# Half of one modulation vector's product moved from the attention stage to the output projection

## The chip, the cores and the metric

The kernel runs on one core of a Trainium2 chip. A core has TensorE (matmuls), VectorE, ScalarE, GpSimd and SyncE (called PE, DVE, ACT, POOL and SP in the profile), each with its own queue of instructions that it takes in order, and 16 DMA engines that move data between HBM and the core's on-chip memory. The metric is the device time of one execution in microseconds. Work on different engines overlaps; an instruction that waits holds up what stands behind it in its own queue.

## The reference, cut to what matters

One decoder layer over 256 tokens of width 2048: four groups of attention heads, an output projection, then a mixture of 16 experts of which each token takes two. A vector `c` of the sequence gives six modulation vectors of 2048 numbers each.

```python
c_act = jax.nn.silu(c)
mod = c_act @ ada_w[l] + ada_b[l]
sh1, sc1, g1, sh2, sc2, g2 = jnp.split(mod, 6, axis=-1)
h = rmsnorm(x, norm1_g[l]) * (1.0 + sc1[:, None]) + sh1[:, None]
x = x + g1[:, None] * token_mixer(h, w_in[l], ...)
h = rmsnorm(x, norm2_g[l]) * (1.0 + sc2[:, None]) + sh2[:, None]
x = x + g2[:, None] * moe_ffn(h, router_w, router_bias, ...)
return rmsnorm(x, final_g)
```

`g2` scales what the experts give, so it is wanted last of the six. Its weights are 2048 x 2048 numbers in float32, 16.8 MB.

## The kernel before

All weights are streamed from HBM once, in one list of units of 512 KB (128 partitions x 1024 numbers; the expert gate and up weights in units of 1 MB). The class `Stream` gives each unit a slot in on-chip memory as slots come free (`pump`, `done`) and SP issues the loads. Slots are halves of the ring tiles `r0` to `r4`, a single `r5` and, once attention no longer needs them, the tiles `T` of the position biases and a few more. Names as `ug`, `uo`, `uw`, `ugu` in the profile are such slots, named after the unit that took them first.

The stages follow each other, and the list of units has their order:

1. The vectors `sc1` and `sh1` and the first projections of w_in (until about 158 us).
2. The other projections of w_in, 69 units, and attention for the groups D, C, A and B. A unit of w_in is split into a high part `whi` (ScalarE, line 584) and a low part `wlo` (VectorE, line 586), and three matmuls (lines 561 to 563, or 565 to 567) take the place of one. `order` mixes the units of w_in with those of `sc2`, `sh2` and `g2`, evenly.
3. The output projection: 32 pieces of w_out (`opieces`, counted from 0), split in the same way, two pieces ahead of the matmuls `oacc` (`SPLITS = 2`). `order2` mixes the pieces with the units of `g1`. After every eight pieces, 512 columns of `x` are added up (lines 1190 and 1191); the last 512 columns come in two halves. Then the router picks the experts.
4. Eight pairs of experts, gate, up and down weights. In the first pair, the columns of `g2` are spread to rows of `g2r` by `spread`, among the gate and up matmuls.

A vector in `VEC` is made on VectorE: `ada_acc_v` takes 1024 columns at a time and adds one unit (128 rows of the weight) after another to `ada_v`: the first by a product (line 509), the others by a multiply-add (line 511). `ada_item` calls it for each unit, and after the sixteenth puts the finishing on a list, `late_cols`; `finish_cols` calls `ada_finish`, which sums over the partitions with small matmuls and a transposition (`ada_cols`). A tuple of 16 units is one block, so `sc2`, `sh2` and `g2` make six blocks of 16 units.

The order within each engine's queue is set when the kernel is built: a scheduler takes the instructions as written and places them by a simulated timeline, so a change in the list of units moves neighbours too.

Of the kernel before, what the change touches and what calls it, by code (L numbers as in the profile page):

```python
# [11 lines left out]
F32 = mybir.dt.float32  # L12
# [8 lines left out]
D = 2048  # L21
S = 256
KC = D // 128
# [2 lines left out]
F = 512  # L26
CAP = 64
VEC = {(n, h) for n in ("sc2", "sh2", "g2") for h in range(2)}
TAIL = ("g1",)
NEG = -1e30  # L30
EPS = 1e-6
TINY = float(np.finfo(np.float32).tiny)
# [1 line left out]
UNIT = 1024  # L34
# [146 lines left out]
def hybrid_trunk_kernel(  # L181
# [113 lines left out]
    def ada_blocks(nm):  # L295
        return [k for h in range(2) for k in ([(nm, 2 * h, 1024)] if (nm, h) in VEC else
                                              [(nm, 2 * h, 512), (nm, 2 * h + 1, 512)])]
# [11 lines left out]

    nw = len(wtiles)  # L310
    wkeys = [u[0] for i in range(NEARLY, nw) for u in win_units(i)[3 * (i == SIXTH):]]
    blocks = [k for nm in ("sc2", "g1", "sh2", "g2") if nm not in TAIL for k in ada_blocks(nm)]
    lines = [[(k, u) for k in blocks if k[2] == width for u in range(KC * width // UNIT)] for width in (1024, 512)]
    akeys = [a[1:] for a in sorted(((n + 0.5 * on) / (len(ks) + 1), *ku)
                                   for on, ks in enumerate(lines) for n, ku in enumerate(ks))]
# [16 lines left out]
            units.append(ada_block(it[1])[it[2]])  # L332
    opieces = [(n, u) for n, us in WORDER for u in us]
    order2, fi = [], 0
    akeys2 = [(k, u) for nm in TAIL for k in ada_blocks(nm) for u in range(KC * k[2] // UNIT)]
    for i in range(32):
        order2.append(("o",) + opieces[i])
        while fi < len(akeys2) and fi < 1.2 * i + AHEAD:
            order2.append(("a",) + akeys2[fi])
            fi += 1  # L340
    order2 += [("a",) + k for k in akeys2[fi:]]
    for it in order2:
        units.append(wout_units(it[1])[it[2]] if it[0] == "o" else ada_block(it[1])[it[2]])
# [184 lines left out]
    def spread(cols, dst):  # L528

        pr = ps("PT", [128, 4, 128], name="ada_r")  # L530
        for i in range(4):
            dg = small([128, 128], "dg", bufs=2)
            V.tensor_scalar(dg, ident, cols[:, i:i + 1], None, OP.mult)
            mm(pr[:, i, :], ones[:], dg[:], start=True, stop=True)
        A.copy(dst, pr[:].rearrange("p i n -> p (i n)"))
# [7 lines left out]
    g2c = const.tile([128, KC], F32, name="g2c")  # L543
# [545 lines left out]
    def finish_cols(age):  # L1089
        for c in late_cols:  # L1090
            c[0] += 1
        while late_cols and late_cols[0][0] > age:
            late_cols.pop(0)[1]()
# [5 lines left out]
    for it in order:  # L1099
        if it[0] == "w":  # L1100
            i, u = pieces[pn]
# [44 lines left out]
    late = wrA = bsb = rt = xt = g1b = fa8 = selb = tms = x1q = None  # L1146
# [277 lines left out]
    next(first)  # L1424
    ssy = const.tile([128, 2, 7], F32, name="ssy")
    fgr = []
    for p in range(NP):
        xg = xgs[p // 2]
        gp = ps("mm", [128, 512], name="gatep")
        up = ps("mm", [128, 512], name="upp")  # L1430
        for n, (c, g) in enumerate(GUORDER):
            if n == 5:
                weights(p)
            if p == 0 and n > 3:

                b = n - 4
                if b == 0:
                    g2r = late.tile([128, D], F32, name="g2r", tag="g2r")
                spread(g2c[:, 4 * b:4 * b + 4], g2r[:, 512 * b:512 * b + 512])
            o = (gp, up)[g]  # L1440
            keys = [(("gu", p), c, g, e) for e in range(2)]
            bt = Batch()
            for i in range(4):
                k = 4 * c + i
                if not p and not g and not i % 2:
                    next(first, None)
                if not p or i == 2:
                    bt = Batch()
                for e in (1, 0):
                    w = stream.get(keys[e])[:, 512 * i:512 * i + 512]  # L1450
                    s0 = 2 * CAP * (p % 2) + CAP * e
                    bt(mm, o[64 * e:64 * e + 64, :], xg[:, k, s0:s0 + CAP], w, start=k == 0, stop=k == KC - 1)
            for key in keys:
                stream.done(key)
# [218 lines left out]
```

## Time and profile before

| | |
|---|---|
| median of 3 runs | 1056.02 us (1053.86 to 1061.72) |
| profiled execution | 1056.39 us |
| its span, first to last instruction | 1054.6 us |
| TensorE busy | 960.3 us (91%) |
| VectorE busy | 500.4 us (47%) |
| ScalarE busy | 353.1 us (33%) |
| moved by DMA | 371.14 MB, mean 352 GB/s |

The busy times come from one execution and are averages over stages that differ. Matmuls are pipelined and their ends are modelled, so a busy TensorE isn't TensorE at its peak. The chain of waits is followed back from the last instruction; "issue" in it is time in which an engine waited for nothing that the profile shows. The DMA share is the mean busy share of the 16 DMA engines; it can pass 1.

### The profile page before, as it was taken

The page shows a single profiled execution, that of the slowest core. Times are in us where ns is not written, and L with a number is a line of the kernel's source. Part 1 is how long each engine was busy: PE and PEld are TensorE (multiplying, and loading weights), DVE is VectorE, ACT ScalarE, POOL GpSimd, SP SyncE. Part 2 cuts the span into 40 slices and gives each one's busy share as a digit, 9 for nine tenths or more (in the row PEclk, how much of TensorE's full clock was granted, in tenths as well). Part 3 has the DMA queues.
Part 4 walks back from the last instruction along what each step waited for, and adds up shares of the span by engine and source line. Part 5 has one row for each costly group of instructions (what it writes and reads, how often), then busy time and mean ns, then how long its engine had stood idle before and what let it go on. Part 6 is the DMA issues. An engine that isn't in the chain of part 4 may idle for free.

```text
span 1054.6 us, 16417 instructions
## 1 busy us (share of the span) xinstructions
PE 960.3 (91%) x6465; PEld 582.9 (55%) x6465; DVE 500.4 (47%) x1006; ACT 353.1 (33%) x763; POOL 4.8 (0%) x14
## 2 busy tenths in 40 slices
PE   5899999999999998989998999999889897899994
PEld 1677778898788985656784433433243232433323
DVE  2444566996998998344445231414024040422215
ACT  3333344566776768534444101100010000200013
POOL 0000000000000000000000000000000000000000
PEclk9999999999999999999998999999999999999998
DMA  9999999996999999889653999999999999999994
GB/s 332 357 358 359 357 323 325 355 373 210 335 325 348 325 384 387 307 270 384 228 214 145 341 421 414 412 417 415 422 407 421 412 420 413 419 419 414 421 359 128
DMA packets 153596, 371.14 MB, mean 352 GB/s; under 512 B 11514, under 2 KB 90275, under 8 KB 136875
## 3 DMA queue, kind: packets, MB, share of 16 engines
q1 hardware_dynamic: 152512, 368.41, 94.2%
q10 hardware_dynamic: 938, 1.61, 0.4%
q8 instruction: 53, 0.87, 0.3%
q14 instruction: 29, 0.23, 0.1%
q0 software_dynamic: 64, 0.02, 0.0%
HBM read 367.91 MB, written 2.10 MB: 351 GB/s over the span
## 4 chain that ended last, share of the span: by engine, by line
PE 66%; DMA 15%; DVE 8%; ACT 5%; issue 4%; SPq 0%; DVEq 0%; ACTq 0%
PE dn L201 10%; DMA ugu<-in_exp_w_up_dram 9%; PE acc L561 5%; PE acc L562 4%; PE acc L563 4%; PE gatep L201 4%; PE upp L201 3%; PE ada L201 3%; PE upp L204 3%; DMA r<-in_exp_w_up_dram 3%; PE oacc L565 3%; PE pg L1410 3%; PE oacc L566 3%; PE oacc L567 3%; PE gatep L204 2%
## 5 line engine op out<-in xcount | busy, mean ns | idle before, releaser
L561 PE MATMUL acc<-Hh,wlo 128*128 128x256 f32 x512 | 145.7, 294 | 6.3 <-DVE wlo L586 3.9
L562 PE MATMUL acc<-Hl,whi 128*128 128x256 f32 x512 | 146.1, 288 | 0.0
L563 PE MATMUL acc<-Hh,whi 128*128 128x256 f32 x512 | 145.2, 286 | 0.0
L586 DVE TENSOR_TENSOR wlo<-r,whi 128x1024 fp32r<-128x1024 f32 x85 | 103.8, 1221 | 62.7 <-ACT whi L584 60.1
L584 ACT CAST whi<-r 128x1024 fp32r<-128x1024 f32 x85 | 88.9, 1047 | 77.2 <-PE acc L563 28.7
L561 PEld LDWEIGHTS acc<-Hh,wlo 128*128 128x128 f32 x512 | 96.3, 192 | 16.9 <-DVE wlo L586 7.0
L562 PEld LDWEIGHTS acc<-Hl,whi 128*128 128x128 f32 x512 | 98.6, 193 | 3.5 <-issue 2.6
L563 PEld LDWEIGHTS acc<-Hh,whi 128*128 128x128 f32 x512 | 98.6, 193 | 2.7 <-issue 2.3
L511 DVE SCALAR_TENSOR_TENSOR ada_v<-r,cT,ada_v 128x1024 f32<-128x1024 f32 x75 | 95.9, 1279 | 0.4
L204 PE MATMUL upp<-ugu,xg 128*64 128x512 f32 x220 | 90.7, 597 | 4.4 <-DMA ugu<-in_exp_w_up_dram 4.4
L1464 DVE TENSOR_TENSOR he<-upp,sg 128x128 f32<-128x128 f32 x32 | 7.1, 282 | 180.0 <-PE upp L204 180.0
L204 PE MATMUL gatep<-ugu,xg 128*64 128x512 f32 x192 | 82.2, 601 | 0.5 <-DMA ugu<-in_exp_w_gate_dram 0.5
L1543 ACT CAST yhl<-yo 128x512 fp32r<-128x512 f32 x31 | 19.1, 618 | 164.1 <-DVE yo L1537 136.8
L204 PE MATMUL gatep<-r,xg 128*64 128x512 f32 x176 | 71.1, 596 | 0.9 <-DMA r<-in_exp_w_gate_dram 0.9
L201 PE MATMUL dn<-udh,heT 128*64 128x512 f32 x140 | 68.0, 599 | 1.0 <-DVE heT L1481 1.0
L1494 DVE TENSOR_TENSOR xt<-xt,sco 128x512 f32<-128x512 f32 (+1 forms) x70 | 42.1, 637 | 55.4 <-PE sco L1493 54.9
L204 PE MATMUL upp<-r,xg 128*64 128x512 f32 x148 | 65.7, 596 | 2.6 <-DMA r<-in_exp_w_up_dram 2.6
L204 PE MATMUL dn<-udh,heT 128*64 128x512 f32 x140 | 67.6, 599 | 0.0
L1460 ACT ACTIVATE sg<-gatep 128x512 f32<-128x512 f32 x8 | 4.8, 597 | 167.9 <-PE gatep L204 167.9
L565 PE MATMUL oacc<-wlo,Oh 128*128 128x512 f32 (+1 forms) x160 | 58.8, 369 | 0.2
L201 PE MATMUL dn<-r,heT 128*64 128x512 f32 (+1 forms) x124 | 55.5, 558 | 1.6 <-DVE heT L1481 1.6
L567 PE MATMUL oacc<-whi,Oh 128*128 128x512 f32 (+1 forms) x160 | 56.8, 355 | 0.0
(404 smaller groups left out, 1909.0 us busy)
## 6 DMA issues: line engine op xcount, KB each, us to landing
r<-in_ada_w_dram SPq DMA_DIRECT2D x156, 512.0 KB, 7.6
udh<-in_exp_w_down_dram SPq DMA_DIRECT2D x70, 512.0 KB, 11.4
r<-in_w_in_dram SPq DMA_DIRECT2D x69, 512.0 KB, 7.3
ugu<-in_exp_w_up_dram SPq DMA_DIRECT2D x34, 1024.0 KB, 14.6
ugu<-in_exp_w_gate_dram SPq DMA_DIRECT2D x33, 1024.0 KB, 13.8
r<-in_exp_w_gate_dram SPq DMA_DIRECT2D x31, 1024.0 KB, 13.0
r<-in_exp_w_up_dram SPq DMA_DIRECT2D x30, 1024.0 KB, 14.3
r<-in_exp_w_down_dram SPq DMA_DIRECT2D x56, 512.0 KB, 11.4
```

Source lines behind the costliest of these rows:

```text
L201: ins = op(*args, **kw).ins
L204: ins = op(*args, **kw).ins
L511: V.scalar_tensor_tensor(acc, w, cT[:, u:u + 1], acc[:], OP.mult, OP.add)
L561: ins = mm(o, wl, hh, start=first, stop=False)
L562: mm(o, wh, hl, start=False, stop=False)
L563: mm(o, wh, hh, start=False, stop=last)
L565: ins = mm(o, hh, wl, start=first, stop=False)
L566: mm(o, hl, wh, start=False, stop=False)
L567: mm(o, hh, wh, start=False, stop=last)
L584: A.copy(hi, w)
L586: V.tensor_tensor(lo, w, hi[:].bitcast(F32), OP.subtract)
L1494: V.tensor_tensor(y(t, cs), y(t, cs), o, OP.add)
```

## The change

`g2` has two blocks of 1024 columns. The first block (columns 0 to 1023) leaves `order` and enters `order2`: its 16 units follow the pieces of w_out with the numbers 18 to 31, one or two behind each (`G2FROM = 17`). The second block stays where it was. The finishing of the late block is called in the first pair of experts, ahead of the spreading, and the four rows of `g2r` are spread in the order 2, 3, 0, 1.

```diff
-TAIL = ("g1",)
+TAIL = ("g1", "g2")
+G2FROM = 17
...
-    blocks = [k for nm in ("sc2", "g1", "sh2", "g2") if nm not in TAIL for k in ada_blocks(nm)]
+    blocks = [k for nm in ("sc2", "sh2") for k in ada_blocks(nm)] + ada_blocks("g2")[1:]
...
-    akeys2 = [(k, u) for nm in TAIL for k in ada_blocks(nm) for u in range(KC * k[2] // UNIT)]
+    akeys2 = [(k, u) for k in ada_blocks("g1") for u in range(KC * k[2] // UNIT)]
+
+    g2keys = [[(k, u) for u in range(KC)] for k in ada_blocks("g2")]
+    gi = 0
     for i in range(32):
         order2.append(("o",) + opieces[i])
         while fi < len(akeys2) and fi < 1.2 * i + AHEAD:
             order2.append(("a",) + akeys2[fi])
             fi += 1
+        while gi < KC * (i - G2FROM) / (31 - G2FROM):
+            order2.append(("a",) + g2keys[0][gi])
+            gi += 1
...
+    def g2_row(b):
+
+        spread(g2c[:, 4 * b:4 * b + 4], g2r[:, 512 * b:512 * b + 512])
+
...
+            if p == 0 and n == 4:
+                finish_cols(0)
+                g2r = late.tile([128, D], F32, name="g2r", tag="g2r")
             if p == 0 and n > 3:
-
-                b = n - 4
-                if b == 0:
-                    g2r = late.tile([128, D], F32, name="g2r", tag="g2r")
-                spread(g2c[:, 4 * b:4 * b + 4], g2r[:, 512 * b:512 * b + 512])
+                g2_row((2, 3, 0, 1)[n - 4])
```

The lines of the changed kernel have other numbers: 511 is 518 there, 586 is 593, 1190 and 1191 are 1197 and 1198.

First place: SP's queue at the start of the mixed stage, behind the units for the compression in group D. Before (`in_ada_w` with 128x1024 is a unit of `sc2`, `sh2` or `g2`, `in_w_in` one of w_in):

```order
L219 DMA r_96<-in_ada_w_dram 128x1024
L219 DMA r_97<-in_ada_w_dram 128x1024
L237 DMA r_97<-in_w_in_dram 128x4x256
L219 DMA r_98<-in_ada_w_dram 128x1024
L219 DMA r_94<-in_ada_w_dram 128x1024
L237 DMA r_98<-in_w_in_dram 128x4x256
```

Now, in the same place:

```order
L220 DMA r_96<-in_ada_w_dram 128x1024
L238 DMA r_97<-in_w_in_dram 128x4x256
L220 DMA r_97<-in_ada_w_dram 128x1024
L238 DMA r_98<-in_w_in_dram 128x4x256
L220 DMA r_94<-in_ada_w_dram 128x1024
```

Between two units of w_in there is now one unit of the modulation weights where there were two; over the whole stage 80 of 96 are left.

Second place: VectorE's queue in the output projection, from the split of piece 24 to that of piece 28. Before (two `wlo` in a row stand as x2: those of 23 and 24, 25 and 26, 27 and 28; `work` and `xt` are the additions to `x`):

```order
L586 TENSOR_TENSOR wlo<-uo_5467,whi 128x1024 x2
L1190 TENSOR_TENSOR work<-oacc,g1b 128x512 x2
L1191 TENSOR_TENSOR xt<-xt,work 128x512 x2
L586 TENSOR_TENSOR wlo<-r_98,whi 128x1024 x2
L586 TENSOR_TENSOR wlo<-uo_5534,whi 128x1024 x2
```

Now:

```order
L593 TENSOR_TENSOR wlo<-ug_5536,whi 128x1024
L518 SCALAR_TENSOR_TENSOR ada_v<-uo_5563,cT,ada_v 128x1024
L1197 TENSOR_TENSOR work<-oacc,g1b 128x512 x2
L518 SCALAR_TENSOR_TENSOR ada_v<-r_95,cT,ada_v 128x1024
L593 TENSOR_TENSOR wlo<-uo_5563,whi 128x1024
L1198 TENSOR_TENSOR xt<-xt,work 128x512 x2
L518 SCALAR_TENSOR_TENSOR ada_v<-ug_5589,cT,ada_v 128x1024
L593 TENSOR_TENSOR wlo<-r_97,whi 128x1024
L518 SCALAR_TENSOR_TENSOR ada_v<-ug_5596,cT,ada_v 128x1024
L593 TENSOR_TENSOR wlo<-ug_5589,whi 128x1024
L518 SCALAR_TENSOR_TENSOR ada_v<-r_95,cT,ada_v 128x1024
L518 SCALAR_TENSOR_TENSOR ada_v<-r_98,cT,ada_v 128x1024
```

Six of the late sums now stand between these splits, three of them between the splits of pieces 24 and 26, and two in a row ahead of that of piece 28.

Third place: SP's queue at the end of the output projection, up to the first up weights of the experts. Now (the rows of w_out are the last four pieces; before, no row of `in_ada_w` stood among or behind them):

```order
L246 DMA r_96<-in_w_out_dram 128x4x256
L220 DMA ug_5589<-in_ada_w_dram 128x1024
L246 DMA ug_5589<-in_w_out_dram 128x4x256
L246 DMA r_97<-in_w_out_dram 128x4x256
L246 DMA r_94<-in_w_out_dram 128x4x256
L220 DMA ug_5596<-in_ada_w_dram 128x1024
L220 DMA ug_5664<-in_ada_w_dram 128x1024
L260 DMA ug_5664<-in_exp_w_down_dram 128x1024
L220 DMA r_95<-in_ada_w_dram 128x1024
L220 DMA r_96<-in_ada_w_dram 128x1024
L257 DMA ugu_5693<-in_exp_w_up_dram 128x2048
```

Four units of `g2` are the last loads before the experts' up weights, the first of which stood among the pieces of w_out before.

## Rows read from the trace of the kernel before

**Rows 1.** From the profile page: the span, and the busy tenths of TensorE, VectorE and the DMA engines with the GB/s moved, in 40 equal slices of the span (26.4 us each).

```profile
span 1054.6 us, 16417 instructions
...
PE   5899999999999998989998999999889897899994
...
DVE  2444566996998998344445231414024040422215
...
DMA  9999999996999999889653999999999999999994
GB/s 332 357 358 359 357 323 325 355 373 210 335 325 348 325 384 387 307 270 384 228 214 145 341 421 414 412 417 415 422 407 421 412 420 413 419 419 414 421 359 128
```

**Rows 2.** Busy time of each engine by stage: the stretch, its length in us, then us busy (and instructions) of PE, PE's weight loads, DVE, ACT and POOL, the granted clock, the DMA share and GB/s.

```profile
158.00:211.00 53.00, 51.43 (x510) 44.86 (x499) 43.11 (x84) 27.04 (x56) 1.05 (x2) 1.00 1.00 341
211.00:264.00 53.00, 52.33 (x435) 46.03 (x435) 40.98 (x80) 34.02 (x85) 0.00 (x0) 1.00 0.85 291
264.00:422.00 158.00, 147.88 (x1152) 126.53 (x1151) 143.02 (x261) 110.25 (x272) 0.00 (x0) 0.98 1.00 351
422.00:475.00 53.00, 50.12 (x316) 31.07 (x315) 22.18 (x60) 24.59 (x57) 1.68 (x3) 0.93 0.85 288
475.00:527.00 52.00, 52.00 (x270) 37.23 (x269) 23.06 (x25) 23.48 (x37) 0.00 (x0) 1.00 0.85 308
527.00:557.00 30.00, 25.22 (x207) 23.62 (x205) 16.20 (x47) 14.71 (x28) 0.00 (x0) 0.93 0.56 210
557.00:606.00 49.00, 48.40 (x234) 22.69 (x236) 18.60 (x44) 13.79 (x23) 0.00 (x0) 0.94 0.67 244
606.00:1015.00 409.00, 373.15 (x1702) 140.93 (x1699) 102.75 (x197) 35.87 (x61) 0.00 (x0) 1.00 1.02 416
```

**Rows 3.** Two consecutive matmuls of TensorE's timeline in the attention stage: start us, us, engine, line, operation, tiles and shapes.

```profile
330.23 0.28 PE L567 MATMUL acc<-whi,Hh 128*128 128x256 f32 x1
330.35 0.28 PE L565 MATMUL acc<-wlo,Hh 128*128 128x256 f32 x1
```

**Rows 4.** The chain of waits by engine and line, as shares of the stretch: from 158 to 422 us, from 264 to 422 us, and from 475 to 557 us.

```profile
by line: issue 11.5%; PE acc L561 9.0%; PE acc L562 8.0%; PE acc L563 7.9%; DVE ada_v L511 5.8%; DVE wlo L586 4.8%; DMA r<-in_w_in_dram 4.8%; PE acc L565 4.8%; PE acc L566 4.3%; PE acc L567 4.3%; ACT whi L584 4.1%; PE PT L204 2.9%; PE sp L2
...
by line: issue 15.5%; DMA r<-in_w_in_dram 8.1%; DVE ada_v L511 7.1%; ACT whi L584 6.2%; PE acc L561 6.0%; PE acc L562 5.2%; PE acc L563 5.2%; DVE wlo L586 5.0%; DMA r<-in_ada_w_dram 3.2%; PE acc L565 2.8%; DMA uw<-in_w_in_dram 2.8%; PE PT L
...
by line: PE oacc L565 24.4%; PE oacc L566 22.7%; PE oacc L567 22.7%; PE g1p L1065 4.9%; PE ada L201 4.3%; PE PT L1203 3.2%; PE rt L1209 2.6%; PE g1p L1064 2.3%; ACT xh L1369 1.6%; ACT L1297 1.6%; PE lg L1232 1.0%; DVE dg L533 1.0%; PE ada_r
```

**Rows 5.** The instructions that write or read the tile `ada_v`, over the whole span: count, then minimum, median and maximum in ns, the first and the last start in us, and the shapes.

```profile
L511 DVE SCALAR_TENSOR_TENSOR ada_v<-r,cT,ada_v x75: 1254/1279/1286, 150.5 to 409.4; 128x1024 f32<-128x1024 f32 x75
...
L522 DVE STREAM_TRANSPOSE ada_v<-ada_c x6: 443/450/450, 199.9 to 431.5; 128x256 f32<-128x256 f32 x6
...
L509 DVE TENSOR_SCALAR ada_v<-r,cT x5: 744/752/753, 146.8 to 374.9; 128x1024 f32<-128x1024 f32 x5
...
L523 DVE TENSOR_TENSOR A2n<-ada_v,rT x2: 168/169/170, 200.4 to 254.3; 128x8 f32<-128x8 f32 x2
```

**Rows 6.** From the profile page: the loads of the modulation weights that went to ring slots, their number, KB each, and median us from issue to landing.

```profile
r<-in_ada_w_dram SPq DMA_DIRECT2D x156, 512.0 KB, 7.6
```

**Rows 7.** SP's timeline in the output projection: the first loads of `x` and the last pieces of w_out (start us, us until the last of the group was issued).

```profile
467.02 3.06 SPq L1183 DMA_DIRECT2D xt<-in_x_dram  x6
...
498.18 1.74 SPq L245 DMA_DIRECT2D uo<-in_w_out_dram  x2
```

**Rows 8.** VectorE's timeline from the split of piece 24 to that of piece 30; in brackets the idle time before an instruction, and what ended it.

```profile
519.69 1.23 DVE L586 TENSOR_TENSOR wlo<-uo,whi 128x1024 fp32r<-128x1024 f32 x1 [1.50 <-ACT whi L584]
520.84 1.28 DVE L1190 TENSOR_TENSOR work<-oacc,g1b 128x512 f32<-128x512 f32 x2
522.03 1.28 DVE L1191 TENSOR_TENSOR xt<-xt,work 128x512 f32<-128x512 f32 x2
523.24 1.22 DVE L586 TENSOR_TENSOR wlo<-r,whi 128x1024 fp32r<-128x1024 f32 x1
525.35 1.22 DVE L586 TENSOR_TENSOR wlo<-r,whi 128x1024 fp32r<-128x1024 f32 x1 [0.90 <-ACT whi L584]
529.04 1.22 DVE L586 TENSOR_TENSOR wlo<-uo,whi 128x1024 fp32r<-128x1024 f32 x1 [2.46 <-ACT whi L584]
532.67 1.23 DVE L586 TENSOR_TENSOR wlo<-uo,whi 128x1024 fp32r<-128x1024 f32 x1 [2.41 <-ACT whi L584]
533.81 0.42 DVE L1190 TENSOR_TENSOR work<-oacc,g1b 128x256 f32<-128x256 f32 x1
534.48 0.42 DVE L1190 TENSOR_TENSOR work<-oacc,g1b 128x256 f32<-128x256 f32 x1 [0.24 <-PE oacc L567]
534.82 0.75 DVE L1191 TENSOR_TENSOR xt<-xt,work 128x256 f32<-128x256 f32 x2
535.55 1.23 DVE L586 TENSOR_TENSOR wlo<-r,whi 128x1024 fp32r<-128x1024 f32 x1
538.23 0.42 DVE L1229 COPY work<-PT 128x256 f32<-128x256 f32 x1 [1.45 <-PE PT L1227]
539.14 1.22 DVE L586 TENSOR_TENSOR wlo<-uo,whi 128x1024 fp32r<-128x1024 f32 x1 [0.48 <-ACT whi L584]
```

**Rows 9.** Who waited for whom: VectorE's longest wait from 475 to 548 us, and SP's from 475 to 575 us (us in total, times, longest).

```profile
DVE wlo L586 <- ACT whi L584: 35.7, 14, 5.4
...
SPq L256 <- DVE wlo L586: 27.5, 7, 6.3
```

## The prediction

> **What bounds the kernel now.** The page comes first. TensorE is busy for 91% of the span and the DMA row shows a 9 in nearly every slice; the slices that don't are the tenth and those from the 17th to the 22nd, and the GB/s line has its holes there [rows 1]. The table by stage puts figures on them [rows 2]. From 158 to 422 us (projections and attention) the transfers run at a share of 0.85 to 1.00, VectorE is busy for 227 of 264 us and TensorE for 95%. That 95% isn't a limit: matmuls of this stage have records of 0.28 us and start 0.12 us apart [rows 3], so busy records overlap and hide waits. From 422 to 557 us (output projection, router) transfers fall to 288, 308 and 210 GB/s and VectorE is busy for 45% of the time. From 606 us on (the experts) transfers run at 416 GB/s with a share of 1.02, to the end.
>
> The chain of waits says who sets the pace [rows 4]. In attention no engine does: matmuls, "issue", the sums of `ada_v`, the splitting into `wlo` and `whi`, and transfers take turns. From 264 to 422 us alone, transfers are 8.1 + 3.2 + 2.8 = 14.1% of the chain and `ada_v` is 7.1%. From 475 to 557 us some 70% of the chain is the `oacc` matmuls: TensorE sets the pace, and VectorE waits for ScalarE's split, which waits for TensorE (35.7 us in 14 waits) [rows 9].
>
> So the same work is on the path, in part, where the change takes it from, and beside it where the change puts it, if it fits.
>
> **What leaves the attention stage.** Of six blocks of 16 early sums one goes: one opening product of 0.75 us and 15 sums of 1.279 us [rows 5], 0.75 + 15 x 1.279 = 19.9 us of VectorE. With them go 16 transfers of 512 KB [rows 6], 8.39 MB. On the path are only parts of both:
> - Sums: `ada_v` is 5.8% of the chain over 264 us [rows 4], 15.3 us; a sixth of the sums go, so 2.6 us.
> - Transfers: 14.1% of 158 us is 22.3 us of chain from 264 us on. If these waits shrink with the bytes (8.39 of the stage's 337 GB/s x 264 us = 89 MB, 9.4%; the rate is from the stage table's first three rows), 2.1 us go. If each landing comes earlier by all that is no longer ahead of it, all 22.3 us can go. Queues near their limit shorten faster than their load, which speaks for more than 2.1; the 15.5% "issue" and the splits in the same chain, which stay, speak for far less than 22.3. I take 6 us.
> - Bounds for both together: nothing, if the split-multiply loop keeps its pace; 25 us, if transfers alone set it (8.39 MB at 337 GB/s).
>
> Gain taken: 2.6 + 6 = 8.6 us.
>
> **What enters the output projection.** VectorE gets the 19.9 us here: two of the sums ahead of the split of piece 12, the other 14 behind the splits of pieces 16 to 29. A split `wlo` can start only when ScalarE's `whi` is there, and the idle time before each shows what fits [rows 8]. Taking the new order of VectorE's rows against those gaps: a sum of 1.28 us fits into idle 1.50, 2.46 and 1.45 + 0.48. It doesn't fit around 520 to 525 us, where the four additions of `work` and `xt` fill the gap: three sums stand there against 0.90 idle, 3 x 1.28 - 0.90 = 2.9 us over. Two sums in a row against 2.41 are 0.15 over. One sum beside the additions of 533.81 to 535.55 us, with 0.24 idle among them, is 1.04 over, less one addition of 0.37 us (half of the last pair) that now comes later: 0.7. TensorE waits for each of these, since its next piece needs `wlo`. Cost: 3.8 us. Bounds: nothing, if the two buffers of `wlo` take up the delay; 19.9 us, if every sum delays a split.
>
> The finishing of this half (a transposition of 0.45 us and an addition of 0.17 us [rows 5], after eight small matmuls) leaves a busy stage and now stands between the last addition and the router's first reduction on VectorE: 0.6 us, on the path. Bounds: nothing and about 1.5 us with the wait for the matmuls.
>
> The transfers: SP issues 14 of the 16 units behind the loads of `x`, mixed with the last 12 pieces of w_out, ahead of all expert weights but the first gate pair and one down unit. They cost nothing here if they land before VectorE reaches them. The cover is the hole: from 475 to 557 us transfers stay under the experts' rate by (416 - 308) x 52 + (416 - 210) x 30 = 11.8 MB, and SP mostly waits there for a slot (27.5 us for `wlo`) [rows 2, 9]. 14 units are 7.3 MB. Without that cover they would cost 8.39 MB / 416 GB/s = 20.2 us. Expert weights are prefetched later, into slots that come free by the last split as before; the first pair of experts starts then, with the same slots full. `spread` makes the same four rows of `g2r` in another order: nothing.
>
> **The sum.** The profiled execution took 1056.39 us (span 1054.6, 1.8 around it), 0.4 above the median of the runs. 1056.4 - 8.6 + 3.8 + 0.6 = 1052.2: **1052 us**.
>
> **Rivals.**
> - *Attention is limited by its transfers.* For it: shares of 1.00 from 158 to 211 and from 264 to 422 us, beside 1.02 where the experts stream, and SP far from idle. Then the units that leave (16 in 264 us, 12.8 of them in these 211 us) give back their transfer time, 12.8 x 0.524 MB / 348 GB/s = 19 us: 1056.4 - 19 + 4.4 = 1042 us. Against it: 416 GB/s in the expert stage shows that the engines move more than 351. A rule of the Trainium skill (DMA: Bandwidth & Descriptors, Specifications) gives one core's share of HBM as about 358 GB/s and calls that side the binding one; by it attention sits at the ceiling and 8.39 MB would be worth 23 us, an estimate from that page. The 416 GB/s of this trace contradict it as a ceiling. Chance 0.23.
> - *Attention keeps its pace.* The loop of split, `wlo` and matmul, with TensorE at 95%, is the limit, and what leaves was waiting beside it: 1056.4 + 4.4 = 1061 us. For it: "issue" and matmuls are over half of the chain. Against: 14% of the chain are transfers. Chance 0.15.
> - *The late sums wait for their data* (the slower side). VectorE takes its rows in order; a sum whose unit hasn't landed holds the split behind it, and so TensorE and every slot that SP waits for. From the first loads of `x` on, at 467 us [rows 7], the change queues 30 units of 512 KB, 2.1 MB of gates, 2.1 MB of `x` and one down unit of 0.5 MB: 20.4 MB, wanted by the split at 539 us, so 283 GB/s. The stage before ran at 288 and the next at 308 [rows 2]; the margin is thin. At 250 GB/s the queue needs 82 us, 10 too many: 1062. At 210 GB/s, the rate of 527 to 557 us, it needs 97, 25 too many: 1077. It decides below about 234 GB/s, where the queue comes 15 us late and the time passes 1067. Against it: these rates are low because slots weren't free (in the kernel before, the last piece is issued at 498 us, and SP then waits for splits [rows 7, 9]), and a summed unit frees its slot at once. Chance 0.15.
>
> That the change doesn't do what it says is excluded by the order: 80 of the 96 sums are early, 16 late.
>
> **Chances.** Forecast 0.47, rivals 0.23, 0.15, 0.15. One per cent is 10.6 us, about what a measurement of this kernel can tell from no change. Faster by over 1% (under 1046): most of the first rival (0.20) and the good edge of my case (0.08), 0.28. Slower by over 1% (over 1067): 0.13 of the third rival and 0.01 of the second, 0.14. Within: 0.58. The range reaches from 1041, just under the first rival's value, to 1064, past the second rival and into the third; half of the first rival's chance and most of the third's lie outside.
>
> **What would show it.** Right: 80 `ada_v` operations in attention and 16 late; what now stands at 422 us comes near 413; transfers are a smaller part of its chain; pieces 16 to 29 take some 4 us more, with VectorE near 85% busy; transfers over 350 GB/s from 475 to 557 us; the experts' stretch keeps its 409 us at 416 GB/s. Wrong on the gain: the chain of attention keeps its length and shows "issue" or ScalarE where transfers were. Wrong on the cost: `ada_v` waits for a transfer between 500 and 545 us, `oacc` matmuls show idle time before them put down to `wlo`, or the first expert pair waits for up weights, which are now the last to be issued before it.

## The result: slower by 1.1%, and the profile after

The changed kernel took 1068.19 us (median of 4 runs, 1066.15 to 1071.15), the kernel before 1055.95 us beside it (4 runs). The ratio is 1.0108, with a 95% interval of 1.0079 to 1.0137. The forecast was 1052 us with a range up to 1064; the change made the kernel slower, and by more than the range allowed. The profiled execution of the changed kernel took 1067.70 us, its span 11.0 us more than before.

From the page of the changed kernel, the rows that answer to [rows 1] (slices of 26.6 us):

```profile
span 1065.6 us, 16414 instructions
...
PE   5999999799999998989998998999789998899885
...
DMA  9999998698699997879983999999999999999992
GB/s 336 358 359 358 357 312 282 223 371 271 190 348 342 374 357 269 294 231 398 384 316 141 342 421 415 417 419 406 423 412 411 412 419 416 416 420 414 421 377 102
```

The eighth slice (186 to 213 us) is new: 223 GB/s where there were 355, and TensorE's digit falls to 7. In the 20th and 21st slices, the output projection, the transfers reach 384 and 316 GB/s where they had 228 and 214, so that hole is filled as forecast. Others have opened: the 16th slice has 269 where it had 387.

The same by stage, in the stretches of [rows 2] (length, then us busy of PE, its weight loads, DVE, ACT and POOL, granted clock, DMA share, GB/s):

```profile
158.00:211.00 53.00, 43.93 (x421) 37.80 (x410) 33.22 (x64) 24.09 (x44) 1.06 (x2) 0.87 0.75 251
211.00:264.00 53.00, 52.91 (x438) 46.80 (x437) 44.12 (x77) 35.01 (x84) 0.00 (x0) 1.00 0.94 324
264.00:422.00 158.00, 151.16 (x1208) 130.35 (x1208) 130.75 (x261) 112.63 (x283) 0.00 (x0) 0.98 0.91 319
422.00:475.00 53.00, 50.25 (x321) 32.86 (x319) 24.83 (x61) 25.70 (x60) 1.68 (x3) 1.00 0.73 244
475.00:527.00 52.00, 51.20 (x238) 31.83 (x239) 27.81 (x30) 21.54 (x31) 0.00 (x0) 0.97 1.04 381
...
606.00:1015.00 409.00, 376.60 (x1704) 143.05 (x1702) 105.02 (x206) 36.58 (x61) 0.00 (x0) 0.99 1.02 415
```

TensorE does 421 instructions from 158 to 211 us where it did 510. From 264 us on it does more than before (1208 against 1152), but it starts that far behind.

A few first and last starts in the traces say where the 11 us come from. `vC` and `qkC` are the tiles to which C's v and its q and k are written, `qkA` the same for A; `perm` is the first matmul that permutes `A2n` after attention, and `gatep` the first gate matmul of the experts.

| us | before | changed | difference |
|---|---|---|---|
| `vC`, last | 230.3 | 243.8 | +13.5 |
| `qkC`, last | 248.3 | 259.4 | +11.1 |
| `qkA`, last | 354.3 | 355.8 | +1.5 |
| `perm`, first | 465.5 | 470.9 | +5.4 |
| `gatep`, first | 561.2 | 569.8 | +8.6 |
| last store of `out` | 1048.6 | 1059.7 | +11.1 |

Some 12 us are lost within 40 us of group D's stage. A's last q and k come nearly on time again, but only because A's projections now stand earlier in TensorE's order: the first scores of A (`sp` from `qkA`) start at 344.1 us where they started at 326.9. Counted in matmuls, the changed kernel is 95 behind at 264 us (2348 against 2443), 38 behind at 354 us (3078 against 3116) and 38 behind at 422 us (3554 against 3592). At 0.12 us each that is some 5 us, about what `perm` is late by. So some 7 of the 12 us come back. The output projection and router add 3.2 us, the experts 2.5.

What happens in group D is in the chain of waits from 184 to 211 us of the changed kernel (start, us, what):

```profile
193.08 0.38 PE scmp L859 x4
193.56 0.61 DVE pc L868 x4
...
196.61 1.28 ACT L831
198.11 1.28 ACT L877
...
200.71 0.27 DVE cst L881
201.21 0.48 DVE pc L884 x2
...
203.60 0.31 DVE vc L850
204.04 1.10 PE pcTp L890 x4
```

This is the compression of D's keys and values: small steps that alternate between VectorE and ScalarE (the two rows of 1.28 us are loads of ScalarE's activation table). TensorE's timeline of the same kernel ends so (in brackets the idle time and what ended it):

```profile
196.75 0.71 PE L205 MATMUL sp<-qkD 64*128 64x128 f32 x5
198.15 0.44 PE L845 MATMUL vcp<-pk,hT 128*15 128x64 f32 x16 [0.69 <-ACT hT L831]
204.04 1.09 PE L890 MATMUL pcTp<-ident,pc 128*128 128x128 f32 x4 [5.46 <-DVE vc L850]
```

Between `vcp` and `pcTp` no matmul of a w_in piece stands in TensorE's queue. Before there were 73, three pieces of w_in:

```profile
191.04 0.44 PE L838 MATMUL vcp<-pk,hT 128*15 128x64 f32 x16
...
202.71 0.60 PE L883 MATMUL pcTp<-ident,pc 128*128 128x128 f32 x4
```

The two steps lie 5.9 us apart now and lay 11.7 us apart before, and `pcTp` starts only 1.3 us later than it did. So the chain isn't longer; the work beside it is gone. A smaller stall comes ahead of it. ScalarE's split waits 5.6 us for a piece of w_in until 179.4 us, and the step behind it in ScalarE's queue holds up TensorE:

```profile
182.03 0.31 PE L836 MATMUL kcp<-hT,pk 128*64 128x30 f32 x4 [2.13 <-ACT hT L831]
```

With that, `vcp` starts 7.1 us later than before. The stretch 193 to 205 us, before and then changed:

```profile
193.00:205.00 12.00, 10.56 (x90) 9.31 (x90) 11.46 (x26) 8.28 (x21) 0.00 (x0) 1.00 1.04 376
```

```profile
193.00:205.00 12.00, 5.85 (x59) 4.90 (x57) 6.05 (x29) 7.72 (x16) 0.00 (x0) 0.79 0.47 167
205.00:211.00 6.00, 5.21 (x26) 4.25 (x26) 5.79 (x6) 2.07 (x5) 0.00 (x0) 0.56 0.47 141
```

SP issues nothing from 193.2 to 207.0 us and the transfers fall to 167 GB/s; after the idle time the granted clock is 0.56 from 205 to 211 us, near the lower of its two levels (1.2 of 2.4 GHz); before, it was 1.00 from 158 to 264 us [rows 2]. Matmuls that stood 0.12 us apart start 0.21 us apart here, from 207.63 us on.

### The profile page after: what moved, and what is told of

Its sections match the earlier page's. It is cut to its first block, busy times and chain, and to the rows that moved or that the text cites. A ratio compares the mean times of both kernels' runs of the same rounds, so it can differ in the third digit from the quotient of the medians.

```text
span 1065.6 us, 16414 instructions
## 1 busy us (share of the span) xinstructions
PE 970.0 (91%) x6465; PEld 585.7 (55%) x6465; DVE 503.6 (47%) x1006; ACT 356.8 (33%) x765; POOL 4.8 (0%) x14
## 4 chain that ended last, share of the span: by engine, by line
PE 70%; DMA 17%; DVE 7%; ACT 4%; issue 2%; SPq 0%; DVEq 0%; ACTq 0%
PE dn L202 11%; DMA r<-in_exp_w_up_dram 7%; PE acc L568 5%; PE acc L569 5%; PE acc L570 5%; PE gatep L202 4%; PE upp L202 4%; PE ada L202 4%; DMA r<-in_exp_w_gate_dram 3%; PE pg L1417 3%; PE upp L205 3%; PE gatep L205 3%; DMA r<-in_ada_w_dram 3%; PE oacc L572 3%; PE oacc L573 2%; PE oacc L574 2%
## 5 line engine op out<-in xcount | busy, mean ns | idle before, releaser
L518 DVE SCALAR_TENSOR_TENSOR ada_v<-r,cT,ada_v 128x1024 f32<-128x1024 f32 x71 | 90.8, 1279 | 1.7 <-DMA r<-in_ada_w_dram 1.2
L205 PE MATMUL upp<-ugu,xg 128*64 128x512 f32 x196 | 73.3, 598 | 1.3 <-DMA ugu<-in_exp_w_up_dram 1.3
L205 PE MATMUL gatep<-ugu,xg 128*64 128x512 f32 x200 | 72.1, 601 | 0.5 <-DMA ugu<-in_exp_w_gate_dram 0.5
L202 PE MATMUL dn<-udh,heT 128*64 128x512 f32 x134 | 64.2, 600 | 2.1 <-DVE heT L1492 2.1
L205 PE MATMUL dn<-udh,heT 128*64 128x512 f32 x138 | 65.9, 600 | 0.0
L205 PE MATMUL upp<-r,xg 128*64 128x512 f32 x172 | 62.9, 595 | 1.4 <-DMA r<-in_exp_w_up_dram 1.4
L205 PE MATMUL gatep<-r,xg 128*64 128x512 f32 x168 | 63.4, 624 | 0.0
L573 PE MATMUL oacc<-whi,Ol 128*128 128x512 f32 (+1 forms) x160 | 56.5, 353 | 0.0
## 6 DMA issues: line engine op xcount, KB each, us to landing
ugu<-in_exp_w_up_dram SPq DMA_DIRECT2D x34, 1024.0 KB, 14.1
```

What stands on the lines that cost most here:

```text
L202: ins = op(*args, **kw).ins
L205: ins = op(*args, **kw).ins
L518: V.scalar_tensor_tensor(acc, w, cT[:, u:u + 1], acc[:], OP.mult, OP.add)
L573: mm(o, hl, wh, start=False, stop=False)
```

## The experiments

All differences are to runs of the kernel before on the same chip. Its median was 1055.78 us beside runs 1 to 5, 1057.21 beside 6 to 9, 1055.86 beside 10 to 12, 1057.27 beside 13 and 14, and 1057.41 beside 15 and 16; the ratios are those on record and differ from the quotients of the medians by up to 0.2% (second run: 1.0100). The theory after the first look (A): the forecast gain in C and A is there, and the uncovered compression hides it. The rival (B): the late sums and their data cost more than forecast. From the sixth run on the letters stand for the theories named in the expectations there.

**1, 2, 3 and 5: each half of the change, and the matmuls at the compression** (there is no fourth run). The first moves the loads of one compression weight behind a later piece of w_in, so that 48 matmuls stand before `pcTp`. The second leaves the late sums out, the third adds late sums to the kernel before, the fifth joins the first two.

```diff
-W1AT = (1, 3)
+W1AT = (1, 4)
```

> The change, with the two units of w1v one piece of w_in later in the list (W1AT 1, 4 instead of 1, 3). In the changed kernel the order of TensorE has no projection matmul between the last of the compression and the probabilities' transposition pcTp, where the kernel before has 73, and the trace shows TensorE idle there; with this edit 48 stand there again. Theory A (the loss is this new order around the compression): pcTp no longer has an idle stretch before it, the last vC comes near 231 us instead of 244, and the time falls by 8 to 12 us, to 1056 to 1060. Theory B (the loss is the late sums and their transfers in the output projection): the start of attention changes, but its end and the time don't: 1066 to 1070.

```diff
-            order2.append(("a",) + g2keys[0][gi])
             gi += 1
...
+    V.memset(g2c[:, 0:8], 1.0)
```

> The change without the late block: the first half of the columns of g2 is neither loaded nor summed, and ones stand in its place. The early part is that of the changed kernel. Theory A: the loads of x still come near 473 us, not 467, and the time is 1056 to 1062, no better than the kernel before although 8.4 MB are missing. Theory B: everything the change lost was in the late part; without it the forecast gain is there: 1045 to 1049.

```diff
-    blocks = [k for nm in ("sc2", "sh2") for k in ada_blocks(nm)] + ada_blocks("g2")[1:]
+    blocks = [k for nm in ("sc2", "sh2") for k in ada_blocks(nm)] + ada_blocks("g2")
...
-    g2keys = [[(k, u) for u in range(KC)] for k in ada_blocks("g2")]
+    g2keys = [[(k, u) for u in range(KC)] for k in [("g2x", 0, 1024)]]
```

> The kernel before with all six blocks early as they were, and the first block of g2 loaded and summed a second time where the change puts it, into columns that nothing reads. The early order is that of the kernel before. Theory A: only the cost of the late part shows, 4 to 6 us: 1060 to 1062. Theory B: the whole loss and the gain that should have been beside it show: 12 to 20 us, 1068 to 1076.

> Both edits: the late block left out (ones in the place of the first half of g2) and w1v one piece later. This shows what the removal gives attention when the order around the compression doesn't spoil it. Theory A: 8 to 10 us less than the run without the late block alone, 1045 to 1050. Theory B: the same as that run, within 3 us.

| run | us | ratio to before (95%) |
|---|---|---|
| 1: compression weight later | 1062.23 | 1.0051 (1.0027 to 1.0075) |
| 2: early part only | 1066.34 | 1.0080 (1.0050 to 1.0111) |
| 3: late part only | 1059.28 | 1.0024 (1.0002 to 1.0046) |
| 5: early part only, weight later | 1062.90 | 1.0053 (1.0030 to 1.0076) |

The rival falls: the late part, even with 8.4 MB more to transfer, costs 0.24%, 2.5 us (3.5 by the medians). Taking work away costs 0.8%. Covering part of the compression gives back 6 us, about half; but with no late sums it gives only 3.4 (fifth against second), so something else in the early part is lost as well. Theory A's own figures were missed: the first run lies between the two theories, the second above both, and the fifth 13 us above the 1050 us that A allowed.

**6 to 9: sums, loads, and the places of the units that stay.** The line `(f + FRONT * f * (1 - f)) * len(akeys)` spreads the early units evenly over the pieces. With 80 units for 96, every unit that stays gets a new place, and the D stage gets fewer of them. The next four runs keep the old places: with the sums alone cut, with the loads alone cut, with the early block gone, and with the whole change. In all four 73 matmuls stand before `pcTp`, as in the kernel before. The edit of the last (the third leaves the late sums out besides):

```diff
-    blocks = [k for nm in ("sc2", "sh2") for k in ada_blocks(nm)] + ada_blocks("g2")[1:]
+    blocks = [k for nm in ("sc2", "sh2", "g2") for k in ada_blocks(nm)]
...
-            order.append(("a",) + akeys[fi])
+            if akeys[fi][0][:2] != ("g2", 0):
+                order.append(("a",) + akeys[fi])
             fi += 1
```

The core of the first two, both on the kernel before (`c` is column 0 alone for the block; `own` marks its sums, which have no load):

```diff
-            V.scalar_tensor_tensor(acc, w, cT[:, u:u + 1], acc[:], OP.mult, OP.add)
+            V.scalar_tensor_tensor(acc[:, c], w[:, c], cT[:, u:u + 1], acc[:, c], OP.mult, OP.add)
...
+            V.scalar_tensor_tensor(acc, acc[:] if own else w, cT[:, u:u + 1], acc[:], OP.mult, OP.add)
```

> The kernel before with the sixteen early sums of g2's first half cut to one column of 1024; the sixteen units are still loaded, at their old places, and the matmuls around the compression stand as before. Only VectorE is relieved, by about 16 x 1.2 us. Theory A (the early part has room, and the changed kernel lost it because the units that remain were spread anew): VectorE was the smaller part of the forecast gain, 1052 to 1055 us. Theory B (TensorE sets the pace of attention, so that taking VectorE work away gives nothing even in the old order): 1054 to 1058 us. Theory C (VectorE is the limit): under 1050 us.

> The kernel before with the sixteen loads of g2's first half left out and the sixteen sums kept at their places, each adding the accumulator to itself; only the transfers are relieved, by 16 units of 512 KiB. Theory A: transfers were the larger part of the forecast gain (6 us), 1047 to 1052 us. Theory B (TensorE sets the pace): 1054 to 1058 us. Theory C (VectorE is the limit): 1053 to 1057 us.

> The changed kernel without the late sums (g2's first half left at one, as in the second experiment), and with the units of sc2, sh2 and g2's second half at the places that they have in the kernel before, so that 73 matmuls stand between the two steps of the compression again. Theory A (the loss is the new spreading of the remaining units): 1043 to 1050 us, 16 to 23 under the second experiment's 1066. Theory B (TensorE sets the pace, nothing to gain): 1054 to 1058 us. If neither spreading nor TensorE is the cause, the 1066 of the second experiment comes back.

> The whole change, late sums included, with the remaining early units at the places that they have in the kernel before. Theory A: the kernel of the run beside it plus the 3.5 us that the late sums cost, 1046 to 1054 us, faster than before and the forecast of 1052 made good. Theory B: 1057 to 1062 us. If spreading is not the cause, the changed kernel's 1066 to 1070 comes back.

| run | us | ratio to before (95%) |
|---|---|---|
| 6: sums cut | 1058.22 | 0.9997 (0.9977 to 1.0017) |
| 7: loads cut | 1057.93 | 1.0016 (0.9994 to 1.0037) |
| 8: early part only, old places | 1060.59 | 1.0039 (1.0018 to 1.0059) |
| 9: whole change, old places | 1059.65 | 1.0023 (0.9999 to 1.0047) |

Old places bring the whole change from 1.0108 back to 1.0023. So the new places are the loss. But no gain appears either: neither 16 sums nor 16 loads nor both give anything. Theory B, that TensorE sets the pace, had said so, though the sixth and eighth runs lie 0.2 and 2.6 us above its range. Where the gain went can be seen in the transfers of the ninth run, whose attention ends hardly sooner (`perm` at 464.3 us against 465.5). Before, and then the ninth run:

```profile
385.00:415.00 30.00, 29.64 (x219) 22.48 (x218) 29.71 (x59) 20.30 (x51) 0.00 (x0) 1.00 1.05 386
415.00:475.00 60.00, 53.60 (x328) 33.62 (x327) 25.61 (x67) 31.38 (x74) 1.68 (x3) 0.91 0.88 300
```

```profile
385.00:415.00 30.00, 29.38 (x225) 23.24 (x225) 18.23 (x50) 21.74 (x52) 0.00 (x0) 1.00 0.91 313
415.00:475.00 60.00, 52.67 (x318) 37.51 (x316) 29.67 (x69) 32.40 (x77) 1.68 (x3) 0.94 0.65 213
475.00:527.00 52.00, 51.30 (x279) 32.06 (x274) 31.76 (x33) 21.44 (x32) 0.00 (x0) 1.00 1.05 392
```

VectorE is relieved from 385 to 415 us (18.23 us busy against 29.71 before), but nothing moves up; from 415 to 475 us the transfers then stand at 213 GB/s (300 before), and what moved fills 475 to 527. The hole has moved, it isn't closed.

**10 to 12: TensorE relieved, and the new places alone.** The tenth run cuts a third of the matmuls of the last 24 pieces in the kernel before, the eleventh does so in the eighth run's kernel. The twelfth gives the kernel before the changed kernel's places, with all loads kept and, nearly as in the sixth, the sums of the block cut to eight columns.

```diff
-            mm(o, wh, hl, start=False, stop=False)
+            if full:
+                mm(o, wh, hl, start=False, stop=False)
```

> The kernel before, with the middle one of the three split products (high half of w_in by low half of h) left out in the last 24 of the 58 pieces of w_in, from about 320 us on: 192 matmuls less, 20 to 24 us of TensorE at the 0.107 to 0.126 us a matmul takes there. Loads and VectorE's sums stay. Theory B (TensorE alone sets the pace of attention): the first row of the output permutation comes 15 to 24 us before the 465.5 of the kernel before. Theory D (TensorE, VectorE's splits and sums, and the transfers end within a few us of each other, so that relieving one does little): it comes 0 to 6 us before, 1051 to 1058 us in all. In both the whole time falls by less than the stage, since the experts are held to the transfers.

> The same matmuls left out, and also the sixteen early units of g2's first half, with the other units at their old places (as in the eighth experiment; g2's first half stays at one). Theory B: little more than the tenth alone, since loads and sums were not the limit. Theory D: now all three are relieved, and the permutation comes 12 to 20 us before the 465.5, well beyond the sum of the eighth (2.7 us) and the tenth; 1040 to 1052 us.

```diff
+    five = [k for k in akeys if k[0][:2] != ("g2", 0)]
+    at = sorted([(i / len(five), *k) for i, k in enumerate(five)] +
+                [(i / len(akeys), *k) for i, k in enumerate(akeys) if k not in five])
+    akeys = [k[1:] for k in at]
...
-        while fi < len(akeys) and fi < (f + FRONT * f * (1 - f)) * len(akeys):
+        while fi < len(akeys) and at[fi][0] < f + FRONT * f * (1 - f):
```

> The kernel before with the sixteen units of g2's first half still loaded at their old places (their sums cut to eight columns, as good as the sixth experiment), but with the units of sc2, sh2 and g2's second half spread over the whole early part as in the changed kernel. If the new spreading alone is the cause of the loss: the matmuls between the two steps of the compression fall from 73 to 0 and the time rises to 1063 to 1070 us, against 1058 of the sixth. If the loss needs the removal of the units: 1056 to 1060 us.

| run | us | ratio to before (95%) | first `perm` |
|---|---|---|---|
| 10: matmuls cut | 1064.69 | 1.0084 (1.0057 to 1.0110) | 470.7 |
| 11: matmuls and early part cut | 1041.07 | 0.9852 (0.9827 to 0.9878) | 440.7 |
| 12: new places alone | 1074.33 | 1.0163 (1.0135 to 1.0191) | 481.9 |

The twelfth run shows the loss by itself: with not one unit less to load, the new places cost 16 us against the sixth run (the range expected ended at 1070), and the stretch from 158 to 211 us has the marks of the changed kernel (418 matmuls, 0.87, 256 GB/s). Of the 16 us, 11.7 are there by the last `vC` (243.5 us against 231.8 in the sixth, 243.8 in the changed kernel). TensorE's order is that of the changed kernel for 2927 matmuls, up to some 340 us; behind them this run loses more than the changed kernel does. The places are those of loads and sums together; the runs don't part the two.

```profile
158.00:211.00 53.00, 44.32 (x418) 38.29 (x411) 33.89 (x64) 23.87 (x44) 1.06 (x2) 0.87 0.76 256
```

The tenth bears out neither B nor D, which both had `perm` at 465.5 or sooner: less TensorE work made the kernel slower. Its chain from 330 to 400 us shows what takes over:

```profile
by line: DMA r<-in_w_in_dram 24.8%; DMA r<-in_ada_w_dram 17.3%; DVE ada_v L511 14.4%; DMA ug<-in_w_in_dram 11.7%; DMA uo<-in_w_out_dram 10.4%; issue 9.7%; ACT whi L586 6.0%; DVE wlo L588 5.7%; DVE oT L1034 1.8%; DVE ada_v L509 1.1%; DVE ada
...
363.69 4.82 DMA r<-in_w_in_dram
368.61 1.05 ACT whi L586
369.68 1.23 DVE wlo L588
370.91 1.21 DVE ada_v L511
372.14 1.30 DVE ada_v L511
373.45 0.33 SPq L219
373.83 8.20 DMA ug<-in_w_in_dram
```

A sum frees a slot, SP issues into it, 5 to 8 us later the piece lands and is split: transfers are 24.8 + 17.3 + 11.7 + 10.4 = 64% of the chain. Only with matmuls, sums and loads cut together (eleventh) does attention end 24.8 us sooner, against 2.7 for sums and loads alone (eighth run, `perm` at 462.8) and 5.2 later for matmuls alone. That fits theory D: the engines and the queue wait in turns, and one of them alone gives nothing. It isn't shown: in both runs the scheduler also placed the later pieces anew (from some 317 us on TensorE's order differs by more than the matmuls left out), and the fourteenth run below moves `perm` by 20 us through order alone. Why the tenth is slower, and not level, isn't settled.

**13 to 16: how far the old places should go.** The whole change, with the old places over a first part of the 58 pieces of w_in that `order` mixes (here 15%) and even spreading over the rest. (The 69 units in the list of stages are all loads of w_in to ring slots, those of the first stage among them.)

```diff
+    five = [(i / len(akeys), k) for i, k in enumerate(akeys) if k[0][:2] != ("g2", 0)]
+    near = sum(a < 0.15 for a, _ in five)
+    at = [a if i < near else 0.15 + 0.85 * (i - near) / (len(five) - near) for i, (a, _) in enumerate(five)]
+    akeys = [k for _, k in five]
...
-        while fi < len(akeys) and fi < (f + FRONT * f * (1 - f)) * len(akeys):
+        while fi < len(akeys) and at[fi] < f + FRONT * f * (1 - f):
```

> The whole change, with the remaining early units at the places of the kernel before only over the first 15% of the pieces of w_in (D's compression, where 73 matmuls stand between the two steps again), and spread evenly over the other 85%. Theory E (the uncovered compression at 184 to 207 us is the loss by spreading): the last matrix of C (vC) is evacuated within 2 us of the 230 to 232 us of the kernel before and of the ninth, and the time is 1055 to 1061 us. Theory F (the thinner spreading costs all along, through the order of the later pieces): 1063 to 1068 us.

> The same with the old places over the first 33% of the pieces. Theory E: within 2 us of the run beside it. Theory F: between that run and the ninth's 1059.7, that is clearly under the run beside it.

> The whole change with the old places kept over the first 25% of the pieces of w_in. If the places after the compression act smoothly: between the 1054 of 15% and the 1043 of 33%, 1043 to 1054 us. If the 1043 is one lucky order among neighbours: outside that, 1052 to 1062 us.

> The same with 50%. Smoothly: between the 1043 of 33% and the 1060 of 100%, 1043 to 1056 us. One lucky order among neighbours: 1056 to 1064 us.

| old places over | us | ratio to before (95%) | first `perm` |
|---|---|---|---|
| 0 (the change) | 1068.19 | 1.0108 (1.0079 to 1.0137) | 470.9 |
| 15% | 1054.20 | 0.9973 (0.9958 to 0.9989) | 458.5 |
| 25% | 1051.42 | 0.9936 (0.9916 to 0.9957) | 458.2 |
| 33% | 1042.89 | 0.9869 (0.9847 to 0.9891) | 445.3 |
| 50% | 1044.88 | 0.9880 (0.9849 to 0.9910) | 450.9 |
| 100% | 1059.65 | 1.0023 (0.9999 to 1.0047) | 464.3 |

Holding the places up to the compression alone turns 1068 into 1054: TensorE's order is then as before for 2262 matmuls, up to some 245 us, and the 73 matmuls are back. So the places up to the compression are the larger part of the loss, as theory E had it (1055 to 1061 us; its last `vC` near 231 us came at 234.4, in a trace that is 4 us late from 161 us on). That a third would give 11 us more no theory had said. The two neighbours came out inside the ranges set for a smooth effect, so one lucky order is unlikely. At 33% the kernel does all of its work and is 1.3% faster than before. Its stretches:

```profile
264.00:422.00 158.00, 156.55 (x1243) 131.31 (x1240) 129.59 (x271) 120.42 (x309) 0.00 (x0) 1.00 0.95 332
422.00:475.00 53.00, 50.67 (x296) 33.57 (x296) 29.27 (x46) 21.94 (x36) 1.68 (x3) 0.97 0.92 320
475.00:527.00 52.00, 50.47 (x320) 39.80 (x319) 36.33 (x36) 21.26 (x31) 0.00 (x0) 1.00 0.95 353
...
606.00:1015.00 409.00, 373.85 (x1688) 140.83 (x1684) 101.10 (x199) 36.41 (x62) 0.00 (x0) 0.98 1.02 411
```

From 264 to 527 us no stretch has a share under 0.92, where there were two of 0.85 from 422 us on [rows 2]. The chain of the 33% kernel from 264 to 422 us has another look than that of the kernel before [rows 4]:

```profile
by line: PE acc L572 12.0%; PE acc L574 11.0%; PE acc L573 10.9%; PE sp L205 5.7%; PE acc L576 5.5%; PE acc L577 5.1%; DMA uw<-in_w_in_dram 4.9%; PE PT L205 4.9%; PE acc L578 4.8%; PE opv L202 4.7%; PE ada L202 4.6%; issue 3.4%; PE oacc L57
```

The matmuls of w_in (`acc`) are 49% of it, "issue" is 3.4% where it was 15.5%, and one transfer of 4.9% is left among the larger rows where three made 14.1%. In this order it is mostly TensorE that sets the pace. In the ninth run, with the same units gone but the old places, three transfers among the larger rows still make 18% of the chain from 264 to 416 us, where one makes 5.1% here: with the same work, the waits for transfers hang on the order. What this is worth shows in one row of each kernel, the time up to 606 us: before, changed, and 33%.

```profile
0.00:606.00 606.00, 561.75 (x4613) 429.47 (x4615) 378.34 (x761) 306.76 (x674) 4.78 (x14) 0.98 0.93 319
```

```profile
0.00:606.00 606.00, 558.85 (x4569) 427.70 (x4571) 379.00 (x752) 307.91 (x673) 4.78 (x14) 0.97 0.91 313
```

```profile
0.00:606.00 606.00, 571.38 (x4689) 430.88 (x4691) 385.56 (x771) 308.06 (x677) 4.78 (x14) 0.99 0.95 332
```

All three move 371.1 MB in all, and from 606 us on the queue runs at 411 to 416 GB/s. So 6 GB/s less over 606 us are 3.6 MB left over, 9 us at 415 GB/s; the span grew by 11.0. 13 GB/s more are 7.9 MB, 19 us; the span fell by 15.6 (to 1039.0). The same reckoning, from the kernel before, gives the spans of the other kernels to within 4 us, but for runs 2, 7, 8 and 12, which end 6 to 8 us later than it says. It is bookkeeping and names no cause: the end follows the bytes that are not yet there when the experts run, and a change in the early stages is worth, for the most part, what it does to the holes of the queue.

## Why the prediction was wrong, point by point

- **Gain taken, 8.6 us in attention: the step that failed.** The end of attention (`perm`) came 5.4 us later. The working priced the 16 sums and 16 transfers as shares of a chain and took the rest of the stage as unchanged. It wasn't: all 80 remaining units got new places. The rows of SP's queue shown ahead of the prediction had it (one modulation unit between two of w_in where there were two), and 73 matmuls against none between `vcp` and `pcTp` could have been counted. The prediction's check that the change does what it says counted the sums (80 early, 16 late) and not their places. The changed kernel lost 13.5 us by the last `vC`; the twelfth run prices these places, alone, at 16 us, 11.7 of them by then.
- **The size of the gain.** From C's last projection to A's, the changed kernel gains 9.6 us (11.1 late to 1.5 late), which looks like the forecast but is in part A's projections drawn ahead of its scores, and in part lost time caught up. With old places, the gain was 2.7 us without late sums (eighth) and 1.2 with them (ninth), no more than single traces differ by; with the better places, 20.2 us (465.5 to 445.3). The 5.4 us lost lie outside the bounds of the working (nothing to 25 us), the three gains inside them, and 8.6 is near none. The argument that a queue near its limit shortens by more than its load was not borne out: without the 16 transfers alone (seventh) `perm` came 0.6 us sooner. A chain in which engines take turns doesn't say what removing one of them gives.
- **"That 95% isn't a limit."** In the order of the kernel before nothing speaks against it: relieving TensorE alone gave nothing. But with the units gone and better placed, TensorE is next in line, which the working left out: matmuls of w_in are 49% of the fourteenth run's chain, and it was busy for 156.55 of 158 us there.
- **Late sums, 3.8 us, finishing 0.6, late transfers 0: about right.** From `perm` to the first gate matmul the changed kernel takes 98.9 us, before 95.7: 3.2 us. Added alone (third run) the late part costs 2.5 us in all. The transfers fit into the hole, as 1.04 and 381 GB/s from 475 to 527 us show. The sums stood where the order said:

```profile
L518 DVE SCALAR_TENSOR_TENSOR ada_v<-ug,cT,ada_v x7: 1277/1279/1287, 472.6 to 545.3; 128x1024 f32<-128x1024 f32 x7
L518 DVE SCALAR_TENSOR_TENSOR ada_v<-r,cT,ada_v x7: 1276/1277/1285, 506.7 to 542.3; 128x1024 f32<-128x1024 f32 x7
```

- **The experts keep their 409 us: 2.5 us off.** First gate matmul to last store: 487.4 before, 489.9 now, at 415 GB/s.
- **Rivals.** *Transfers limit attention* (1042): the seventh run cuts just these transfers and gains nothing, 1057.93. The 358 GB/s of the Trainium skill named there are again passed, by 415; the same page (DMA: Bandwidth & Descriptors, Bandwidth) gives that figure to a core whose neighbour streams too, which the prediction should have read with it. *Attention keeps its pace* (1061) is what comes out with the old places (1059.65), but its reason, TensorE as the limit in that order, isn't borne out: the tenth run relieved TensorE and was slower. *Late sums wait for their data* (1062 to 1077) would have covered the measured time by another mechanism: over the whole run these sums wait for transfers for 1.4 us in 3 waits, and leaving them out (second run) leaves 1066.34.

The sign thus came from a mechanism that was no case of the prediction: the change does more than it says, since an even spreading depends on how many units are spread.

Open are why the scheduler put nothing between the two steps once units were fewer, why a third is better than 15%, and why the tenth run loses. That the places are the loss is shown (ninth, twelfth and thirteenth run); why the old places leave no gain is argued from the moved hole.

## What to carry to other kernels

When units leave a list that is spread evenly, every other unit moves: compare the order over the whole stage, above all at chains of small dependent steps (count the matmuls beside them, before and after), before pricing the unit that leaves. Where a chain of waits passes from engine to engine, its shares don't add up to a gain; look instead at what the change does to the holes in the transfer queue up to the stage that the queue bounds. And try the places of what stays as a parameter of its own: here it was worth 25 us (1068 to 1043), 14 of them below the kernel before, and the work that was moved takes 20 us of VectorE.

## What the runs showed of the hardware that was not expected

- Idle stretches of TensorE cost more than their length. After the 5.5 us before 204.0 us in the changed kernel the granted clock was 0.56 from 205 to 211 us, with matmuls 0.21 us apart instead of 0.12; after the 2.1 us before 182.0 us it was 0.50, the lower level, from 183 to 186 us, with the same spacing.
- The opening 158 us are nearly the same work in all kernels, yet the granted clock there was 0.97 to 0.99 in some profiles (before, the changed kernel, runs 3, 7, 8, 12 to 15) and 0.89 to 0.91 in the others. The first matmul into `gacc` started between 156.8 us (run 3) and 161.3 (run 13), and not in the order of the clock. Up to it TensorE's order is the same 1492 matmuls in all seventeen traces. So 2 to 4 us between two single traces can be chance, and the verdicts above rest on all runs of a kernel and not on its one trace.
